# Empty tiles that shift where matmul operands start in SBUF, and another tile order in layer 1

## The chip, the core and the metric

The kernel runs on one core of one Trainium2 chip. The metric is the device time of one execution in microseconds (us), the median of several runs. TensorE (PE in the rows) multiplies, VectorE (DVE), ScalarE (ACT) and GpSimd (POOL) do the elementwise work, and every DMA is issued from the queue of SyncE (SP). SBUF holds 128 partitions; a tile has one start offset, the same in every partition, and everything below on offsets speaks of that byte address within a partition.

## The reference

Two layers of a decoder trunk on 1024 tokens of width 1024, in float32:

```python
for l in range(DEPTH):                      # DEPTH = 2
    mk, mv = memory keys and values of layer l, from rms_norm(mem)
    h = rms_norm(x, norm_mix_g[l])
    if l == 0:   # one projection: conv channels | memory queries
        mix = concat(conformer_conv(u[..., :1536] + b), memory_attention(qm, mk, mv))
    else:        # one projection: NSA queries | memory queries | gates
        mix = concat(nsa_attention(q, gates, *shared), memory_attention(qm, mk, mv))
    x = x + mix @ w_out[l]
    x = x + square(relu(rms_norm(x, norm_mlp_g[l]) @ w_mlp_in[l])) @ w_mlp_out[l]
```

`shared` is the keys and values of the three branches of the block-sparse attention (NSA: compressed blocks, selected blocks, sliding window), made once from the stream after layer 0. The MLP is 4096 wide, and most of the arithmetic lies in it.

## The kernel before

**Tiling.** The 1024 tokens are two halves `hf` of 512. Activations lie transposed, 128 channels on the partitions and 512 tokens along the tile, so that 1024 channels are eight tiles `act[kt]`. Every float32 factor is split into a rounded high part and the low rest, both float32r, side by side in one tile of 4096 bytes: `act[kt][:, 0]` high, `act[kt][:, 1]` low; the same for the weights (`hl`), the hidden tiles of the MLP (`hid`), the probabilities (`PT`), and the queries `Q`. One product is then three matmuls, high by high, high by low and low by high (`mm3`, lines 80 to 82). A matmul of 128 by 128 by 512 streams 512 columns of its moving operand (`rhs`) through the array while the stationary operand (`lhsT`) is held; a weight load (PEld) precedes each.

**Which operand moves.** In the first product of the MLP (`ps_i`, lines 452 to 454), in the output projection (`ps_wo`, 411 to 413) and in the projections of layer 0 (`ps_a`, 80 to 82) `act` moves and `hl` stands. In the second product of the MLP (`ps_mo`, 80 to 82) `hid` moves and `hl` stands. In the memory's keys and values (`ps_mkv`, 277 to 279) `hl` moves and `mh` stands. In the projections of the attention (`ps_tok`, 693 to 695; the memory queries of layer 0 at 80 to 82) `hl` moves with 256 columns and `act` stands. In the attention `KS` moves against `Q` (`ps_s`, 1016), `PT` moves against `V` (`ps_o`, 1076 and 1079), and transposes (`ps_t`, 1060) stream `ident` against `prob`.

**Where tiles lie.** Pools are stacked: those on the left from low addresses upwards in the order in which they are opened, those on the right from the top downwards. A pool takes exactly what its tiles need, so each tile's start follows from the sizes of all pools opened before it. The pool `w` (weights, with three `raw` tiles for arriving weights and five `hl` tiles) starts at byte 4928, `hid` follows at 31552, then `tmp`, then `act` at 62464. The slots of `act` serve again as `prob` while the attention of that half runs. Above `act` lie some constants and the residual stream `x`, whose slots also serve as `q`, `mq` and others in the attention. On the right lie the attention's own pools: `wa` (its weights, also called `hl`) and `nsa` (`KS`, `V`, `Q`, `PT`, `sm`, `small`).

**Order.** The program is written with generators, and a scheduler fixes each engine's order when the kernel is built; the engines run their lists in order and meet at semaphores. The stages of PE are: layer 0's projections with the convolution on the other engines (0 to 250 us), output projection and MLP of half 0, then the attention of half 0 and the output projection and MLP of half 1 woven into each other, the attention of half 1 woven into the last MLP of half 0, and at the end output projection and MLP of half 1.

**Layer 1's mixed tiles.** Attention writes its results to DRAM (`mixd`, line 1083): first the memory heads, tiles 6 and 7, then per group of heads tiles 0 to 2 and tiles 3 to 5. `load_mix` (391) reads the eight tiles back in a given order, `w_out` uses them in that order, and the MLP takes the tiles in the same order, since `w_out` puts its result into the slot that came free.

Of the kernel before, what the change touches and what calls it, by code (L numbers as in the profile page):

```python
# [8 lines left out]
F32 = mybir.dt.float32  # L9
# [10 lines left out]
WG = 2  # L20
MIXORD = (4, 5, 6, 7, 0, 1, 2, 3)
MIXORD0 = (0, 1, 2, 3, 4, 5, 6, 7)
SUBP = (0, 2)
ORDER = "B0A1M0X0B1A2A3B2A4B3A5B4B5F0M1Z0G0N1"
MQB = 2
MB = (1, 2)
P = 128
# [359 lines left out]
def load_mix(k, act, src, kts, pool, tag="raw", bufs=2):  # L387

    for kt in kts:
        raw = pool.tile([P, HF], F32, tag=tag, name="mix", bufs=bufs)  # L390
        k.nc.sync.dma_start(raw, src[:, kt])
        split(k.nc, act[kt][:, 0], act[kt][:, 1], raw)
# [237 lines left out]
def mem_dst(mixd, hf):  # L630

    return lambda h, cp: mixd[hf, (h % 2) * 64:(h % 2) * 64 + 64, 6 + h // 2, cp * 256:cp * 256 + 256]
# [280 lines left out]
def nsa(k, pool, psum, hf, q, mq, gate, KcS, Vc, masks, Kd, Vd, kvd, pslot, mem_dst, out):  # L913


    nc = k.nc
# [183 lines left out]
                for j in range(3):  # L1100
                    yield query, scores, (c, g, j, KS, V)

    Q = pend = None
    todo = units()
    unit = next(todo)
    while unit:
        now, unit = unit, next(todo, None)
        Q = Q or now[0](*now[2])
        nextQ = unit and unit[0](*unit[2])
        p = now[1](Q, *now[2])  # L1110
        if pend:
            values(*pend)
        Q, pend = nextQ, p
# [3 lines left out]
def attention(k, hf, x, acc, act, slot, pslot, gate, KcS, Vc, hTA, tail, masks, mixd, kvd, Kd, Vd):  # L1117


    nc, tc, ins = k.nc, k.tc, k.i  # L1120
    h = act
    with tc.tile_pool(name=f"psa{hf}", bufs=1, space=bass.MemoryType.PSUM) as k.psum, \
            tc.tile_pool(name=f"wa{hf}", bufs=1, side="right") as k.wpool:
        with tc.tile_pool(name=f"na{hf}", bufs=1, side="right") as k.tmp:
            k.start(norm_steps(k, h, x, [acc], None))
            k.flush()
        with tc.tile_pool(name=f"pa{hf}", bufs=1, side="right") as cp:
            steps = cmp_kv(k, cp, h, hf, slot, KcS, Vc, hTA, tail)
            next(steps)
            mq = slot(3, [P, 2, 4, P], F32, "mq")  # L1130
            pss = proj(k, h, [ins["b_wm"][:, kt * 292:kt * 292 + 292] for kt in range(KT)], C_MIX1, 292)
            for cs, ps in pss:
                nc.vector.tensor_add(gate[:, 4 * hf + cs.start], ps[:, 256:292], k.rows[:, R_GB:R_GB + 36])
            gv = gate[:, 4 * hf:4 * hf + 4]
            nc.scalar.activation(gv, gv, AF.Tanh, scale=0.5)
            nc.vector.tensor_scalar(gv, gv, 0.5, 0.5, op0=ALU.mult, op1=ALU.add)
            queries(k, cp, [(cs, ps[:, :256]) for cs, ps in pss], by_pair(mq), k.mqg[:, 1])
            next(steps)
            kv_tok(k, h, hf, cp, 0, Kd, Vd)
            next(steps)  # L1140
            next(steps)
            kv_tok(k, h, hf, cp, 1, Kd, Vd)
            next(steps, None)
            q = [slot(j, [P, 4, 256], F32, "q") for j in range(3)]
            for j in range(3):
                queries(k, cp, proj(k, h, [ins["b_wq"][j, i] for i in range(4)], C_MIX1),
                        [q[j][:, 2 * a:2 * a + 2].rearrange("p c (h d) -> p c h d", d=64) for a in range(2)], k.mqg[:, 2])
    with tc.tile_pool(name=f"nsa{hf}", bufs=1, side="right") as pool, \
            tc.tile_pool(name=f"psn{hf}", bufs=1, space=bass.MemoryType.PSUM) as psum:
        nsa(k, pool, psum, hf, q, mq, gate, KcS[hf], Vc[hf], masks, Kd, Vd, kvd, pslot, mem_dst(mixd, hf), mixd[hf])  # L1150


# [2 lines left out]
def build(tc, ins, out):  # L1155
    nc = tc.nc
    k = K()
# [2 lines left out]

    def pool(es, name, side="left"):
        return es.enter_context(tc.tile_pool(name=name, bufs=1, side=side))

    def psum_pool(name):
        return tc.tile_pool(name=name, bufs=1, space=bass.MemoryType.PSUM)

    with ExitStack() as es:
# [14 lines left out]
        xs = dram.tile([2, P, KT, HF], F32, name="xs")  # L1182
        mixd = dram.tile([2, P, KT, HF], F32, name="mixd")
# [5 lines left out]
        k.hid = pool(es, "hid")  # L1189
        k.tmp = pool(es, "tmp")  # L1190
        k.rpool = k.tmp
        ap = pool(es, "act")

        def act_tiles(hf):
# [46 lines left out]
        hTA = late.tile([P, 2, 64], F32, name="hTA")  # L1241
        tail = late.tile([P, 4, 8], F32, name="tail")
        masks = (late.tile([P, 5 * P], F32, name="edge"), late.tile([P, 8, 64], F32, name="cm"))
        xp = pool(es, "x")

        xslot = [slots(xp, f"x{hf}") for hf in range(2)]
# [69 lines left out]

        act = [act_tiles(hf) for hf in range(2)]
        x = [x_tiles(hf) for hf in range(2)]
        load_mix(k, act[0], mixd[0], MIXORD, k.wpool, "raw", k.nraw)
        k.lo_eng = nc.vector  # L1320
        rs = [w_out(k, 1, act[0], x[0], xs[0], MIXORD)]
        ka.rpool = pool(es, "rb", "right")

        ps3 = es.enter_context(psum_pool("ps3"))
        wb = pool(es, "wb", "right")
        ka.psum, ka.wpool, ka.tmp, ka.tag = ps3, wb, wb, "mm"
        load_mix(ka, act[1], mixd[1], MIXORD, ka.wpool, "mix", 8)
        rs.append(w_out(ka, 1, act[1], x[1], xs[1], MIXORD))
        for hf in range(2):
            if hf == 1:  # L1330
                k.psum, k.nps = ps3, 4
            mlp(k, 1, x[hf], act[hf], rs[hf], lambda o: nc.sync.dma_start(out[hf, :, o], x[hf][o]), MIXORD)
        k.flush()


# [66 lines left out]
```

## Time and profile before

| | us |
|---|---|
| median of 3 runs | 2460.57 (2460.16 to 2464.42) |
| the profiled execution, its own time | 2463.4 |
| its span, first to last instruction | 2461.6 |
| PE busy in the span | 2372.0 (96%) |
| DVE, ACT, POOL busy | 1649.2, 1326.1, 1143.4 |
| share of PE in the chain of work that ended last | 85% |
| share of DVE, DMA and ACT in it | 6%, 3%, 2% |

Busy time of PE is the union of its instructions, each drawn with its whole latency (0.39 us for a matmul of 512 columns), while a new one starts every 0.23 us. How fast PE goes is therefore not read from the busy time but from the distance between the starts of neighbouring matmuls, which the list of instructions in order of time gives to 0.01 us; over a run of n steps the mean is good to 0.01 us / n.

### The profile page before, as it was taken

Reading aid. Unit: us, or ns where it says so; the run is one execution under the profiler, and the core shown is the slowest. Engines: PE = TensorE matmul, PEld = TensorE weight load, DVE = VectorE, ACT = ScalarE, POOL = GpSimd, SP = SyncE. Lnnn points to the kernel's source line nnn. Section 1 sums busy time; section 2 is a strip of 40 time slices with the busy share of each in tenths; the row PEclk is TensorE's granted clock in tenths of the full one; section 3 lists DMA queues with packets and bytes.
Section 4 is the critical chain, followed back from the end, with each engine's and each line's share of the span. In section 5 each row is a group of like instructions: output and inputs, shape, how many; then the busy total and the mean of one; then the engine's idle time right before and its main releaser. Section 6 shows DMA issues by size and latency. Waiting matters only on the chain.

```text
span 2461.6 us, 36812 instructions
## 1 busy us (share of the span) xinstructions
PE 2372.0 (96%) x12098; PEld 1994.3 (81%) x12098; DVE 1649.2 (67%) x3598; ACT 1326.1 (54%) x3002; POOL 1143.4 (46%) x1004
## 2 busy tenths in 40 slices
PE   5998999999998999999999899999999997999999
PEld 4887687888787988888787798888888886888887
DVE  7897576998677567877436856778777864433333
ACT  5575555333556567776434665766667653433332
POOL 2876544544401356565440125566565650344443
PEclk9999999999998999999999999999999998999999
DMA  5212433323344342222335442322222225233233
GB/s 185 80 53 84 153 96 101 101 91 95 122 143 141 97 122 81 88 83 78 115 103 165 145 131 86 107 65 67 81 81 62 66 66 183 78 94 97 92 95 102
DMA packets 157214, 250.87 MB, mean 102 GB/s; under 512 B 17632, under 2 KB 48992, under 8 KB 156512
## 3 DMA queue, kind: packets, MB, share of 16 engines
q1 hardware_dynamic: 157024, 248.52, 32.3%
q8 instruction: 96, 1.57, 0.3%
q14 instruction: 94, 0.77, 0.1%
HBM read 217.52 MB, written 20.45 MB: 97 GB/s over the span
## 4 chain that ended last, share of the span: by engine, by line
PE 85%; DVE 6%; DMA 3%; issue 3%; ACT 2%; POOL 1%; SPq 0%; POOLq 0%; ACTq 0%; DVEq 0%
PE ps_i L452 9%; PE ps_i L453 9%; PE ps_i L454 9%; PE ps_mo L80 9%; PE ps_mo L82 8%; PE ps_mo L81 8%; PE ps_t L1060 4%; PE ps_s L1016 4%; PE ps_o L1076 2%; PE ps_wo L411 2%; PE ps_o L1079 2%; PE ps_wo L412 2%; PE ps_wo L413 2%; PE ps_a L80 2%; PE ps_a L82 2%
## 5 line engine op out<-in xcount | busy, mean ns | idle before, releaser
L112 POOL TENSOR_TENSOR hl<-raw,hl 128x512 fp32r<-128x512 f32 x540 | 696.2, 1300 | 759.0 <-ACT hl L111 736.4
L111 ACT ACTIVATE hl<-raw 128x512 fp32r<-128x512 f32 x648 | 405.4, 630 | 630.1 <-PE ps_i L454 251.6
L474 DVE TENSOR_TENSOR x<-x,ps_mo 128x512 f32<-128x512 f32 x512 | 348.8, 684 | 139.1 <-PE ps_mo L82 136.2
L452 PE MATMUL ps_i<-act,hl 128*128 128x512 f32 x1024 | 408.6, 399 | 7.4 <-DVE x L415 7.2
L80 PE MATMUL ps_mo<-hid,hl 128*128 128x512 f32 x1024 | 407.4, 398 | 4.9 <-DVE x L474 4.5
L454 PE MATMUL ps_i<-act,hl 128*128 128x512 f32 x1024 | 407.2, 398 | 0.0
L453 PE MATMUL ps_i<-act,hl 128*128 128x512 f32 x1024 | 406.6, 397 | 0.0
L82 PE MATMUL ps_mo<-hid,hl 128*128 128x512 f32 x1024 | 400.8, 391 | 0.0
L81 PE MATMUL ps_mo<-hid,hl 128*128 128x512 f32 x1024 | 400.7, 391 | 0.0
L452 PEld LDWEIGHTS ps_i<-act,hl 128*128 128x128 f32 x1024 | 192.8, 188 | 51.9 <-DVE x L415 7.4
L460 DVE SCALAR_TENSOR_TENSOR a<-ps_i,r 128x512 f32<-128x512 f32 x128 | 88.1, 689 | 214.4 <-PE ps_i L454 199.3
L80 PEld LDWEIGHTS ps_mo<-hid,hl 128*128 128x128 f32 x1024 | 192.3, 188 | 46.5 <-DVE x L474 8.3
L454 PEld LDWEIGHTS ps_i<-act,hl 128*128 128x128 f32 x1024 | 192.7, 188 | 44.8 <-issue 0.2
L453 PEld LDWEIGHTS ps_i<-act,hl 128*128 128x128 f32 x1024 | 192.8, 188 | 43.2 <-issue 0.2
L82 PEld LDWEIGHTS ps_mo<-hid,hl 128*128 128x128 f32 x1024 | 192.3, 188 | 41.1
L81 PEld LDWEIGHTS ps_mo<-hid,hl 128*128 128x128 f32 x1024 | 192.6, 188 | 37.4 <-issue 0.5
L1027 ACT ACTIVATE prob<-ps_s,small 128x512 f32<-128x512 f32 (+3 forms) x240 | 141.5, 591 | 80.3 <-DVE small L1025 50.7
L1046 POOL TENSOR_TENSOR prob<-prob,small 128x1024 f32<-128x1024 f32 (+3 forms) x120 | 181.2, 1535 | 1.7 <-DVE small L1040 1.4
L1068 DVE TENSOR_TENSOR PT<-ps_t,PT 128x512 fp32r<-128x512 f32 (+1 forms) x220 | 147.3, 671 | 43.4 <-ACT PT L1064 41.4
L1064 ACT ACTIVATE PT<-ps_t 128x512 fp32r<-128x512 f32 (+1 forms) x256 | 141.6, 566 | 60.4 <-PE ps_t L1060 56.2
L1016 PE MATMUL ps_s<-KS,Q 128*128 128x512 f32 (+5 forms) x552 | 144.1, 360 | 0.0
L120 POOL TENSOR_TENSOR hl<-raw,hl 128x512 fp32r<-128x512 f32 (+1 forms) x32 | 38.5, 1205 | 219.2 <-ACT hl L118 185.5
(298 smaller groups left out, 4790.6 us busy)
## 6 DMA issues: line engine op xcount, KB each, us to landing
raw<-in_w_mlp_in_dram SPq DMA_DIRECT2D x256, 256.0 KB, 2.8
raw<-in_w_mlp_out_dram SPq DMA_DIRECT2D x256, 256.0 KB, 2.9
raw<-in_w_out_dram SPq DMA_DIRECT2D x64, 256.0 KB, 3.4
Q<-Q SPq DMA_DIRECT2D x160, 64.0 KB, 2.0
raw<-in_cmp_w_dram SPq DMA_DIRECT2D x32, 256.0 KB, 2.9
raw<-in_a_w_dram SPq DMA_DIRECT2D x24, 256.0 KB, 2.8
raw<-in_b_wq_dram SPq DMA_DIRECT2D x24, 256.0 KB, 2.7
mixd<-ev SPq DMA_DIRECT2D x80, 64.0 KB, 2.1
```

Of the source, the lines that this page charges most:

```text
L80: nc.tensor.matmul(ps, lhsT=lh, rhs=rh, start=(i == 0), stop=False)
L81: nc.tensor.matmul(ps, lhsT=lh, rhs=rl, start=False, stop=False)
L82: nc.tensor.matmul(ps, lhsT=ll, rhs=rh, start=False, stop=(i == n - 1))
L111: nc.scalar.activation(hl[:, 0, :n], raw[:, :n], AF.Copy)
L112: k.last_lo = k.lo_eng.tensor_tensor(hl[:, 1, :n], raw[:, :n], hl[:, 0, :n].bitcast(F32), op=ALU.subtract)
L452: nc.tensor.matmul(p_, lhsT=wh, rhs=h[kt][:, 0], start=kt == 0, stop=False)
L453: nc.tensor.matmul(p_, lhsT=wh, rhs=h[kt][:, 1], start=False, stop=False)
L454: nc.tensor.matmul(p_, lhsT=wl, rhs=h[kt][:, 0], start=False, stop=kt == KT - 1)
L474: nc.vector.tensor_add(x[o], x[o], ps)
L1016: nc.tensor.matmul(o_, lhsT=lhs, rhs=rhs, start=(n_ == 0), stop=(n_ == len(mms) - 1))
L1046: nc.gpsimd.tensor_tensor(t, t, sc[:, :, None].to_broadcast([P, 2, t.shape[-1]]), op=ALU.mult)
L1068: nc.vector.tensor_sub(PT[:, 1, :m], Tv[:, :m], PT[:, 0, :m].bitcast(F32))
```

## The change

Empty tiles are put in front of pools, so that what lies behind them starts elsewhere. `lay0`, 832 bytes, comes before `act`; `lay1`, 768 bytes, before `x`; `lay2` and `lay4`, 160 bytes each, before the attention's pools on the right; `lay5`, 544 bytes, inside `nsa`. Nothing reads or writes them. The numbers below are start offsets modulo 1024 bytes as the two built programs have them (low parts, 2048 bytes on, have the same; slices of 128 columns step by 512 bytes).

| tile | before | after | tile | before | after |
|---|---|---|---|---|---|
| hl of pool w, hid, mh | 832 | 832 | Q in the attention | 512 | 832 |
| act, and prob in its slots | 0 | 832 | KS in the attention | 256 | 576 |
| x, q, mq and others in its slots | 256 | 832 | V in the attention | 512 | 832 |
| hl of pool wa (attention) | 992 | 832 | PT, sm | 992 | 832 |
| hl of pool pair (layer 0) | 96 | 96 | ident | 992 | 992 |
| hl of pool wb (last output projection) | 928 | 928 | | | |

Beyond the kilobyte the two sides differ: `hl` and `hid` start 832 bytes past a multiple of 2048, `act` before 1024 and after 1856 past one.

The second edit replaces the order 4, 5, 6, 7, 0, 1, 2, 3 by 0, 1, 2, 3, 6, 7, 4, 5 in `load_mix`, `w_out` and `mlp` of layer 1, for both halves. The diff, cut to its core:

```diff
+MIXORD1 = (0, 1, 2, 3, 6, 7, 4, 5)
...
         nextQ = unit and unit[0](*unit[2])
+        lay = lay or pool.tile([P, 136], F32, name="lay5")
         p = now[1](Q, *now[2])
...
+            tc.tile_pool(name=f"lay2{hf}", bufs=1, side="right") as lay, \
             tc.tile_pool(name=f"wa{hf}", bufs=1, side="right") as k.wpool:
+        lay.tile([P, 40], F32, name="lay2")
...
+    with tc.tile_pool(name=f"lay4{hf}", bufs=1, side="right") as lay, \
+            tc.tile_pool(name=f"nsa{hf}", bufs=1, side="right") as pool, \
...
+        lay.tile([P, 40], F32, name="lay4")
...
+    def lay(es, size, name, side="left"):
+        if size:
+            pool(es, name, side).tile([P, size // 4], F32, name=name)
...
+        lay(es, 832, "lay0")
         ap = pool(es, "act")
...
+        lay(es, 768, "lay1")
         xp = pool(es, "x")
...
-        load_mix(k, act[0], mixd[0], MIXORD, k.wpool, "raw", k.nraw)
+        load_mix(k, act[0], mixd[0], MIXORD1, k.wpool, "raw", k.nraw)
...
-        rs = [w_out(k, 1, act[0], x[0], xs[0], MIXORD)]
+        rs = [w_out(k, 1, act[0], x[0], xs[0], MIXORD1)]
...
-        load_mix(ka, act[1], mixd[1], MIXORD, ka.wpool, "mix", 8)
-        rs.append(w_out(ka, 1, act[1], x[1], xs[1], MIXORD))
+        load_mix(ka, act[1], mixd[1], MIXORD1, ka.wpool, "mix", 8)
+        rs.append(w_out(ka, 1, act[1], x[1], xs[1], MIXORD1))
...
-            mlp(k, 1, x[hf], act[hf], rs[hf], lambda o: nc.sync.dma_start(out[hf, :, o], x[hf][o]), MIXORD)
+            mlp(k, 1, x[hf], act[hf], rs[hf], lambda o: nc.sync.dma_start(out[hf, :, o], x[hf][o]), MIXORD1)
```

Set side by side, the two built programs have on each engine the same instructions in the same order, and every wait names the same semaphore and the same value; only tile names and addresses differ. Two places show the renaming.

SP's queue after the attention of half 1, before: `mixd<-ev` is the attention's last result, the `mix` rows are the loads of layer 1's tiles 4, 5, 6, 7, 0, 1, 2, 3 (the number in `mix` and `ev` is the allocation's), the bracket names the semaphores waited for.

```order
L1083 DMA mixd_74<-ev_18476 64x2x128 [waits DMAHW7_49,DVE_49]
L108 DMA raw_22073<-in_w_mlp_in_dram 128x512 [waits DMAHW0_49,Pool_49]
L1332 DMA out_0_dram<-x02_18500 128x512 [waits DMAHW1_49,DVE_49]
L391 DMA mix_18890<-mixd_74 128x512 [waits DMAHW7_49,DMAHW2_49,Activation_49]
L391 DMA mix_18894<-mixd_74 128x512 [waits DMAHW3_49]
L391 DMA mix_18898<-mixd_74 128x512 [waits DMAHW4_49]
```

The same place after, where the loads are of tiles 0, 1, 2, 3, 6, 7, 4, 5:

```order
L1084 DMA mixd_74<-ev_18505 64x2x128 [waits DMAHW7_49,DVE_49]
L109 DMA raw_22103<-in_w_mlp_in_dram 128x512 [waits DMAHW0_49,Pool_49]
L1345 DMA out_0_dram<-x02_18530 128x512 [waits DMAHW1_49,DVE_49]
L392 DMA mix_18920<-mixd_74 128x512 [waits DMAHW7_49,DMAHW2_49,Activation_49]
L392 DMA mix_18924<-mixd_74 128x512 [waits DMAHW3_49]
L392 DMA mix_18928<-mixd_74 128x512 [waits DMAHW4_49]
```

Nothing moved: the first load still stands behind the last result and still waits for its landing (`DMAHW7`, to the same count).

ACT at the same place, which makes the high parts of the loaded tiles (`act1x` is tile x of half 1), before:

```order
L87 ACTIVATE act14_18494<-mix_18890 128x512
L87 ACTIVATE act15_18495<-mix_18894 128x512
L87 ACTIVATE act16_18496<-mix_18898 128x512
L87 ACTIVATE act17_18497<-mix_18902 128x512
L87 ACTIVATE act10_18490<-mix_18906 128x512
```

And after:

```order
L88 ACTIVATE act10_18520<-mix_18920 128x512
L88 ACTIVATE act11_18521<-mix_18924 128x512
L88 ACTIVATE act12_18522<-mix_18928 128x512
L88 ACTIVATE act13_18523<-mix_18932 128x512
L88 ACTIVATE act16_18526<-mix_18936 128x512
```

Here the tiles have changed places, and the rows have not: the matmuls of `w_out` follow them in the same way, on the same rows of PE's list.

## Rows read from the trace of the kernel before

**Rows 1.** PE by line and shape: count | busy us, mean ns | idle before and releaser.

```profile
L452 PE MATMUL ps_i<-act,hl 128*128 128x512 f32 x1024 | 408.6, 399 | 7.4 <-DVE x L415 7.2 <-DVE x L474 0.3
...
L1076 PE MATMUL ps_o<-PT,V 128*128 128x256 f32 x396 | 105.7, 285 | 0.0
...
L412 PE MATMUL ps_wo<-act,hl 128*128 128x512 f32 x256 | 104.1, 408 | 0.0
...
L694 PE MATMUL ps_tok<-hl,act 128*128 128x256 f32 x320 | 90.0, 282 | 1.0 <-POOL hl L120 1.0
...
L81 PE MATMUL ps_a<-act,hl 128*128 128x512 f32 x192 | 76.8, 400 | 0.0
```

**Rows 2.** Timeline of PE in the last stage, proj_in: start, us, line, tiles.

```profile
2203.78 0.39 PE L452 MATMUL ps_i<-act,hl 128*128 128x512 f32 x1
...
2214.98 0.39 PE L80 MATMUL ps_mo<-hid,hl 128*128 128x512 f32 x1
```

**Rows 3.** Timeline of PE in the same chunk, proj_out.

```profile
2216.81 0.39 PE L82 MATMUL ps_mo<-hid,hl 128*128 128x512 f32 x1
...
2225.65 0.39 PE L82 MATMUL ps_mo<-hid,hl 128*128 128x512 f32 x1
```

**Rows 4.** Timeline of PE, the memory's keys and values in layer 0.

```profile
28.18 0.39 PE L277 MATMUL ps_mkv<-hl,mh 128*128 128x512 f32 x1
...
32.72 0.39 PE L279 MATMUL ps_mkv<-hl,mh 128*128 128x512 f32 x1
```

**Rows 5.** Timeline of PE, the last output projection.

```profile
2062.28 0.39 PE L411 MATMUL ps_wo<-act,hl 128*128 128x512 f32 x1
...
2102.41 0.39 PE L452 MATMUL ps_i<-act,hl 128*128 128x512 f32 x1
```

**Rows 6.** Timeline of PE, memory queries of layer 0, 256 columns.

```profile
84.94 0.28 PE L82 MATMUL ps_tok<-hl,act 128*128 128x256 f32 x1
...
86.07 0.28 PE L80 MATMUL ps_tok<-hl,act 128*128 128x256 f32 x1
...
87.50 0.28 PE L80 MATMUL ps_tok<-hl,act 128*128 128x256 f32 x1
...
88.92 0.28 PE L80 MATMUL ps_tok<-hl,act 128*128 128x256 f32 x1
```

**Rows 7.** Timeline of PE, a projection of the attention, 256 columns.

```profile
753.41 0.28 PE L693 MATMUL ps_tok<-hl,act 128*128 128x256 f32 x1
...
756.25 0.28 PE L693 MATMUL ps_tok<-hl,act 128*128 128x256 f32 x1
```

**Rows 8.** Timeline of PE where attention and MLP are woven, after transposes.

```profile
1710.71 0.40 PE L81 MATMUL ps_mo<-hid,hl 128*128 128x512 f32 x1
...
1711.87 0.63 PE L1016 MATMUL ps_s<-KS,Q 128*128 128x512 f32 x2
...
1713.63 0.39 PE L82 MATMUL ps_mo<-hid,hl 128*128 128x512 f32 x1
...
1714.53 0.28 PE L1076 MATMUL ps_o<-PT,V 128*128 128x256 f32 x1
```

**Rows 9.** Stretches, matmuls of ps_i alone: us, PE busy (count), PEclk granted, DMA.

```profile
440.00:700.00 260.00, 113.61 (x480) 0.99 0.35 110
1160.00:1300.00 140.00, 68.58 (x288) 1.00 0.36 110
1300.00:2050.00 750.00, 197.68 (x768) 0.99 0.31 96
2050.00:2462.00 412.00, 182.42 (x768) 0.98 0.31 101
```

**Rows 10.** Stretches, matmuls of ps_mo alone, same columns.

```profile
1300.00:2050.00 750.00, 208.36 (x804) 0.99 0.31 96
2050.00:2462.00 412.00, 176.83 (x768) 0.98 0.31 101
```

**Rows 11.** SP's queue after the last attention: start, us, issues.

```profile
2042.87 3.65 SPq L391 DMA_DIRECT2D mix<-mixd  x8
```

More of the change, by code (lines that the diff above doesn't have):

```diff
@@ L1101, in units @@
                     yield query, scores, (c, g, j, KS, V)
-    Q = pend = None
+    Q = pend = lay = None
     todo = units()
@@ L1147, in attention @@
                         [q[j][:, 2 * a:2 * a + 2].rearrange("p c (h d) -> p c h d", d=64) for a in range(2)], k.mqg[:, 2])
-    with tc.tile_pool(name=f"nsa{hf}", bufs=1, side="right") as pool, \
+    with tc.tile_pool(name=f"lay4{hf}", bufs=1, side="right") as lay, \
+            tc.tile_pool(name=f"nsa{hf}", bufs=1, side="right") as pool, \
             tc.tile_pool(name=f"psn{hf}", bufs=1, space=bass.MemoryType.PSUM) as psum:
+        lay.tile([P, 40], F32, name="lay4")
         nsa(k, pool, psum, hf, q, mq, gate, KcS[hf], Vc[hf], masks, Kd, Vd, kvd, pslot, mem_dst(mixd, hf), mixd[hf])
```

## The prediction

> **What bounds the kernel now.** I looked first at the chain of work that ended last: PE holds 85% of it, and in the span PE is busy 96%, with no other engine above 67%. So the question is not who waits for whom but how fast PE goes while it goes. The table of PE's groups [rows 1] gives the counts (three lines of a product, equal in number) and shows that PE hardly idles: 7.4 us before L452, nothing before L412 and L81. Its column of means (399, 408, 400 ns) is latency, not pace. For the pace I went to the timeline of PE and divided the distance of two starts by the steps between them, in stretches that hold one product only.
>
> In the last stage, 48 steps of ps_i take 2214.98 - 2203.78 = 11.20 us, 233.3 ns each [rows 2]. In the same chunk, 39 steps of ps_mo take 2225.65 - 2216.81 = 8.84 us, 226.7 ns each [rows 3]. Both are 512 columns, both have `hl` of pool w standing, and neither run contains a wait. At the full 2.4 GHz, which the granted clock of 0.98 to 1.00 shows for such stretches [rows 9], 512 columns are 213.3 ns; the excess is 13.3 ns in one and 20 in the other. What differs is the moving operand: `hid` starts 832 bytes past a KB, `act` at a whole KB.
>
> Three more places let me sort the causes. In ps_mkv `hl` moves and `mh` stands, both at 832: 20 steps in 4.54 us, 227.0 ns [rows 4]. That product sums 24 matmuls in a PSUM bank as ps_i does, so the length of the sum is not what sets the pace. In the last output projection `act` moves at 0 while `hl` stands at 928: 172 steps in 40.13 us, 233.3 ns [rows 5], so shifting the standing operand by 96 bytes does not help a mover at 0. And in the memory queries, 256 columns with `act` standing at 0, three runs follow each other [rows 6]: `hl` moving at 832, 10 steps, 113.0 ns; `hl` of the pair pool moving at 96, 12 steps, 119.2 ns; `hl` at 832 again, but behind the disturbed run, 12 steps, 118.3 ns. So 832 is no guarantee when the other operand lies at 0: a fast pace exists there, and a disturbance can end it. The same shows where attention and MLP are woven: `hid` at 832 on `hl` at 832 goes at 232.0 ns just after transposes (5 steps, 1.16 us) and at 225 ns, give or take 2.5 for rounding, three microseconds on (4 steps, 0.90 us) [rows 8]. I read this as two streams, the moving operand and the next weights, which fall into step when both start 832 past a KB, and need some matmuls to do so.
>
> **The change part by part.** The two programs have the same lists and the same waits, so no work is added or removed; the sum is of paces alone.
>
> First, ps_i in unbroken stretches. From 440 to 700, 1160 to 1300 and 2050 to 2462 us lie 480 + 288 + 768 = 1536 of them [rows 9]. `act` goes from 0 to 832 and stands against the same `hl` as `hid` does, so I take 233.3 - 226.7 = 6.67 ns: 1536 x 6.67 = **10.2 us**.
>
> Second, ps_i elsewhere: 3 x 1024 [rows 1] less 1536 leaves 1536, woven with attention or convolution. In such a stretch busy time per matmul is 197.68 / 768 = 257.4 ns for ps_i and 208.36 / 804 = 259.2 for ps_mo, so `hid` at 832 has no lead there, whereas in the last stage it has 237.5 against 230.2 [rows 9, 10]. These are busy times with latency in them, and ps_mo waits for a bank every six matmuls, so they only say that the lead is smaller. Bounds 0 and 1536 x 6.67 = 10.2; since `prob`, `V`, `Q` and `PT` come to 832 too and disturb less, I take somewhat over half, **6.0 us**.
>
> Third, ps_wo, 3 x 256 = 768, and ps_a, 3 x 192 = 576 [rows 1]. Of these 192 ps_wo stand on `hl` at 928 and 240 ps_a on `hl` at 96 (the second part of five channel tiles, two halves, 24 each); with a mover at 832 no row shows those pairs. The other 912 give 912 x 6.67 = 6.1 us; the 432 give 0 to 2.9, I take half. Together **7.5 us**. Layer 0's ps_a lies on the path, as PE has no idle time before L81 [rows 1].
>
> Fourth, the attention's projections: 3 x 320 = 960 of 256 columns [rows 1], now at 24 steps in 2.84 us, 118.3 ns [rows 7], with `hl` at 992 on `act` at 0; afterwards both at 832. Nearest rows: 113.0 if they fall into step, 118.3 if not [rows 6]. Bounds 960 x 5.3 = 5.1 us and 0; they run long and unbroken, I take **3 us**.
>
> Fifth, `PT` on `V`, 2 x 396 = 792 [rows 1], 992 to 832 and 512 or 0 to 832: at most 792 x 5.3 = 4.2 us, at least 0. They come a few at a time between transposes, whose `ident` stays at 992, so I take **1 us**. Sixth, the 1536 ps_mo of the woven stretches, which now meet fewer strange offsets: from 232.0 to 226.7 [rows 8] for at most half of them, 0 to 4 us, **1.5 us**. Scores and smaller products I leave out; `KS` comes to 576, not 832.
>
> The order of layer 1's tiles is costed at nothing. An early start of the eight loads could be worth at most their issue time, 3.65 us [rows 11], but the first load stands behind the attention's last result and waits for its landing in either program, and no instruction changes its place.
>
> Sum: 10.2 + 6.0 + 7.5 + 3 + 1 + 1.5 = 29.2 us. It all lies on PE, and what is late next has room: DVE is busy 67%, ACT 54%, POOL 46%. The profiled execution took 2463.4 us with a span of 2461.6, 2.8 us over the median of 2460.57; taking 29.2 off the median gives 2431. Low end 10.2 + 6.1 = 16.3 us, 2444; high end 10.2 + 10.2 + 9.0 + 5.1 + 4.2 + 4 = 42.7, 2418.
>
> **The rivals.** *The offset is not the cause.* The fast movers also lie low (`hl` from byte 4928, `hid` and `mh` from 31552) and the slow ones high (`act` from 62464), so the place in SBUF explains [rows 2 to 5] as well, and the shift leaves the place. Against it: in [rows 6] the same low `hl` runs at both paces, so place alone does not fix the pace. Nothing would change then, 2460. The Trainium skill, "TensorE: Matmul & The Clock Gate", Part 2, speaks for this rival: it gives the moving operand and the weight load two independent read ports in SBUF, so that loading weights takes no bandwidth from a running matmul. By that rule no pair of offsets could matter. The same page has 512/2.4 + 2.5 = 215.7 ns from start to start whatever the operands' addresses; [rows 2] and [rows 3] show 233.3 and 226.7, so the traces disagree with its figure, and by two amounts.
>
> *The new pair is a bad one.* `hl` and `hid` start 832 past a multiple of 2048 bytes, `act` after the change 1856 past one, and no row has that. If what counts is the offset in 2 KB, `act` may land where the pair pool's `hl` is: 119.2 ns for 256 columns [rows 6], 238.4 for 512, 5.1 ns more than now. With 3072 + 768 + 576 = 4416 matmuls that is +22.5 us, 2483. It decides as soon as the pace of ps_i rises above 233.3. Against it: the standing slices of `hl` step by 512 bytes through all of 2048 and [rows 3] keeps one pace over them.
>
> *Only unbroken runs gain.* The woven parts, the projections and the odd pairs give nothing: the low end, 2444.
>
> **How the numbers follow.** Forecast together with its lesser form 0.83, no effect 0.10, the bad pair 0.07. The range 2418 to 2444 is that of the forecast with all its bounds and leaves out the other two, 0.17. A measurement of this kernel tells some 0.2%, 4.9 us, from no change, and every sum of the forecast is beyond that: faster 0.83, same 0.10, slower 0.07.
>
> **What would show it.** Right: starts of ps_i in the last stage 226.7 ns apart, like ps_mo's in the same chunk, and the last stage, 412 us before, shorter by about 768 x 6.67 = 5 us; ps_wo at 226.7; the attention's projections near 113. Wrong: ps_i still at 233.3 (offset not the cause), or above (bad pair); or PE at the new pace with new idle time before L452 and L80, which would mean that something else is late next. SP's loads should start as long after the attention's last result as before; if they come earlier, I misread the queue.

## The result, and the profile after

The changed kernel takes 2444.99 us (median of 6 runs, 2443.32 to 2446.60); the kernel before, run beside it, 2462.1 (6 runs, 2460.16 to 2464.42). The ratio is 0.993, 95% interval 0.9918 to 0.9943: 17 us faster, 0.7%. The forecast was 2431, range 2418 to 2444: the direction is right, the gain of 17.1 us is 0.59 of the 29.2 forecast, and the median lies 1 us above the range.

The profiled execution after took 2443.32 us, 20.1 us less than the one before (2463.4), since it was the fastest of its six. Its page: span, busy time of PE, the share of each engine in the chain that ended last, and the first line of ps_i among PE's groups.

```profile
span 2441.5 us, 36812 instructions
...
PE 2347.9 (96%) x12098; PEld 1993.0 (82%) x12098; DVE 1649.0 (68%) x3598; ACT 1323.7 (54%) x3002; POOL 1145.8 (47%) x1004
...
PE 74%; DMA 4%; DVE 4%; issue 2%; ACT 2%; POOL 1%; SPq 0%; ACTq 0%; POOLq 0%; DVEq 0%
...
L453 PE MATMUL ps_i<-act,hl 128*128 128x512 f32 x1024 | 403.7, 394 | 7.5 <-DVE x L416 7.2
```

PE is still busy 96% of the span, and its share of the chain is still by far the largest, if less than the 85% of before. Its busy time fell by 2372.0 - 2347.9 = 24.1 us; the other engines have the work they had. L453, the first line of ps_i (it was L452), went from 408.6 to 403.7 [rows 1], and its idle time stayed (7.4 and 7.5).

The pace is read as before, from starts in the timeline of PE after. Here is one chunk of the last stage, first ps_i, then ps_mo:

```profile
2187.40 0.39 PE L453 MATMUL ps_i<-act,hl 128*128 128x512 f32 x1
...
2198.28 0.39 PE L81 MATMUL ps_mo<-hid,hl 128*128 128x512 f32 x1
...
2208.94 0.39 PE L83 MATMUL ps_mo<-hid,hl 128*128 128x512 f32 x1
```

48 steps of ps_i take 10.88 us, 226.7 ns each, where [rows 2] had 233.3. ps_mo keeps its 226.7 (47 steps, 10.66 us). `act` has come to the pace of `hid`.

Next, from the same timeline, three products that did not do as forecast: the last output projection (`act` at 832 on `hl` at 928), ps_a on the pair pool's `hl` at 96, and a projection of the attention (256 columns, `hl` at 832 moving on `act` at 832).

```profile
78.58 0.39 PE L81 MATMUL ps_a<-act,hl 128*128 128x512 f32 x1
...
83.94 0.40 PE L83 MATMUL ps_a<-act,hl 128*128 128x512 f32 x1
...
824.38 0.28 PE L694 MATMUL ps_tok<-hl,act 128*128 128x256 f32 x1
...
853.78 0.28 PE L696 MATMUL ps_tok<-hl,act 128*128 128x256 f32 x1
...
2045.67 0.39 PE L414 MATMUL ps_wo<-act,hl 128*128 128x512 f32 x1
...
2087.59 0.40 PE L453 MATMUL ps_i<-act,hl 128*128 128x512 f32 x1
```

The output projection has 41.92 us in 179 steps, 234.2 ns, against 233.3 in [rows 5]: nothing gained. ps_a on `hl` at 96 has 5.36 / 23 = 233.0. The projection takes 29.40 / 245 = 120.0 ns, slower than the 118.3 of [rows 7], and so steady that the 10th and the 90th percentile of its steps both are 120.

The stretches of ps_i and ps_mo after; unlike [rows 9, 10], these lines have two more columns behind PE's, the busy time of the weight loads (PEld) and of DVE. ps_i is in the first fence, ps_mo in the second, and each has the woven stretch ahead of the last output projection and then the last stage:

```profile
1284.00:2034.00 750.00, 192.97 (x768) 139.73 (x768) 21.97 (x32) 0.99 0.31 96
2034.00:2441.00 407.00, 177.46 (x768) 144.07 (x768) 22.02 (x32) 0.99 0.32 103
```

```profile
1284.00:2034.00 750.00, 212.23 (x815) 148.53 (x813) 92.90 (x137) 0.99 0.31 96
2034.00:2441.00 407.00, 176.51 (x768) 144.14 (x768) 87.77 (x128) 0.99 0.32 103
```

The granted clock is 0.99 in both, 0.99 and 0.98 before. In the woven stretch ps_i has 192.97 / 768 = 251.3 ns of busy time per matmul, 6.1 less than before (from start to start the mean fell less there, from 236.8 to 232.6 ns); ps_mo has 212.23 / 815 = 260.4, no less than the 259.2 before. In the last stage ps_i fell from 182.42 to 177.46 us, the 5 us that the prediction gave as a sign.

Last, SP's queue at the second edit's place, and the first ps_wo behind it on PE:

```profile
2023.04 0.59 SPq L1084 DMA_DIRECT2D mixd<-ev  x1
...
2027.32 4.08 SPq L392 DMA_DIRECT2D mix<-mixd  x8
...
2033.21 2.42 SPq L109 DMA_DIRECT2D raw<-in_w_out_dram  x3
```

```profile
2040.05 0.79 PE L412 MATMUL ps_wo<-act,hl 128*128 128x512 f32 x1 [13.96 <-ACT hl L112]
```

The kernel before at the same place, ahead of and behind [rows 11], SP and then PE:

```profile
2038.58 0.59 SPq L1083 DMA_DIRECT2D mixd<-ev  x1
```

```profile
2054.90 0.79 PE L411 MATMUL ps_wo<-act,hl 128*128 128x512 f32 x1 [13.24 <-ACT hl L111]
```

The loads start 4.28 us after the issue of the attention's last result, 4.29 before. But the first ps_wo comes 12.73 us after the loads' start, and came 12.03 us after it before.

### The profile page after: what moved, and what is told of

Its sections match the earlier page's. It is cut to its first block, busy times and chain, and to the rows that moved or that the text cites. A ratio compares the mean times of both kernels' runs of the same rounds, so it can differ in the third digit from the quotient of the medians.

```text
span 2441.5 us, 36812 instructions
## 1 busy us (share of the span) xinstructions
PE 2347.9 (96%) x12098; PEld 1993.0 (82%) x12098; DVE 1649.0 (68%) x3598; ACT 1323.7 (54%) x3002; POOL 1145.8 (47%) x1004
## 4 chain that ended last, share of the span: by engine, by line
PE 74%; DMA 4%; DVE 4%; issue 2%; ACT 2%; POOL 1%; SPq 0%; ACTq 0%; POOLq 0%; DVEq 0%
PE ps_i L453 9%; PE ps_i L455 9%; PE ps_mo L81 9%; PE ps_i L454 9%; PE ps_mo L83 8%; PE ps_mo L82 8%; PE ps_t L1061 4%; PE ps_s L1017 4%; PE ps_o L1077 2%; PE ps_o L1080 2%; PE ps_wo L412 1%; PE ps_wo L413 1%; PE ps_wo L414 1%; PE ps_tok L695 1%; PE ps_tok L696 1%
## 5 line engine op out<-in xcount | busy, mean ns | idle before, releaser
L81 PE MATMUL ps_mo<-hid,hl 128*128 128x512 f32 x1024 | 407.9, 399 | 5.1 <-DVE x L475 4.4
L453 PE MATMUL ps_i<-act,hl 128*128 128x512 f32 x1024 | 403.7, 394 | 7.5 <-DVE x L416 7.2
L455 PE MATMUL ps_i<-act,hl 128*128 128x512 f32 x1024 | 402.3, 393 | 0.0
L454 PE MATMUL ps_i<-act,hl 128*128 128x512 f32 x1024 | 401.5, 392 | 0.0
L453 PEld LDWEIGHTS ps_i<-act,hl 128*128 128x128 f32 x1024 | 192.7, 188 | 46.3 <-DVE x L416 7.4
L81 PEld LDWEIGHTS ps_mo<-hid,hl 128*128 128x128 f32 x1024 | 192.7, 188 | 46.2 <-DVE x L475 8.0
L454 PEld LDWEIGHTS ps_i<-act,hl 128*128 128x128 f32 x1024 | 192.9, 188 | 38.4 <-issue 0.2
```

Source lines behind the costliest of these rows:

```text
L81: nc.tensor.matmul(ps, lhsT=lh, rhs=rh, start=(i == 0), stop=False)
L453: nc.tensor.matmul(p_, lhsT=wh, rhs=h[kt][:, 0], start=kt == 0, stop=False)
L454: nc.tensor.matmul(p_, lhsT=wh, rhs=h[kt][:, 1], start=False, stop=False)
L455: nc.tensor.matmul(p_, lhsT=wl, rhs=h[kt][:, 0], start=False, stop=kt == KT - 1)
```

## The experiments

Unless said otherwise each kernel is the kernel before with the edit shown, timed against it. A mean pace for a product is the mean distance of neighbouring starts over the whole trace, steps of over one and a half times the median left out, so that single waits don't enter.

### Act alone

```diff
+        lay(es, 832, "lay0")
         ap = pool(es, "act")
...
+        lay(es, 192, "lay1")
         late = pool(es, "late")
```

> The kernel before, with act alone moved to 832 bytes past a KB (832 empty bytes ahead of act, 192 behind it, so that everything after lies where it would with a whole KB more). Theory A, the pair of act and hl of pool w makes the whole gain: ps_i in unbroken runs goes from 233.3 to 226.7 ns, its starts add up to about 17 us less, ps_wo and ps_a to about 3 us less, and the time is about 20 us under the kernel before, 2442 us. The attention's projections, with hl still at 992, stay at about 118.3 ns. Theory B, the other empty tiles carry a part of the gain (V, PT, Q, x at 832): at least 5 us are missing, 2447 us or more.

2445.1 us (4 runs, 2440.35 to 2447.22), ratio 0.9925 (0.991 to 0.994): the changed kernel's gain. ps_i in the last stage:

```profile
2126.05 0.39 PE L452 MATMUL ps_i<-act,hl 128*128 128x512 f32 x1
...
2136.71 0.39 PE L454 MATMUL ps_i<-act,hl 128*128 128x512 f32 x1
```

47 steps in 10.66 us, 226.8 ns. The mean pace of ps_i over the whole kernel is 229.9 ns, the same as in the changed kernel, and 235.2 before; ps_wo has 231.5 in both. The projections stay at 118.3. So theory A holds, by the paces and by the time that this kernel shares with the changed one; its 2445.1 us lies between the 2442 and the 2447 of the two theories. `lay0` does it, and the empty tiles ahead of `x`, in `nsa` and ahead of it bring no gain that can be seen, in the woven stretches neither. `prob` lies in the slots of `act` and moved with it here, so what its place adds is not shown.

### The order alone

```diff
-        load_mix(ka, act[1], mixd[1], MIXORD, ka.wpool, "mix", 8)
-        rs.append(w_out(ka, 1, act[1], x[1], xs[1], MIXORD))
+        load_mix(ka, act[1], mixd[1], MIXORD1, ka.wpool, "mix", 8)
+        rs.append(w_out(ka, 1, act[1], x[1], xs[1], MIXORD1))
...
```

> The kernel before, with the order 0, 1, 2, 3, 6, 7, 4, 5 of layer 1's tiles and no empty tiles. Theory A, the order does nothing, since the first of the eight loads waits for the landing of the attention's last result in either program: within 2 us of the kernel before. Theory B, the early tiles come sooner: up to 3.65 us faster, the issue time of the eight loads. A loss of some us would mean that the gain of the empty tiles is larger than the 17 us seen.

2464.02 us (10 runs) against 2462.93 (19 runs), ratio 1.0002 (0.9992 to 1.0011). No gain. SP and PE at the place:

```profile
2043.32 3.65 SPq L392 DMA_DIRECT2D mix<-mixd  x8
...
2048.13 3.61 SPq L109 DMA_DIRECT2D raw<-in_w_out_dram  x3
```

```profile
2056.15 0.80 PE L412 MATMUL ps_wo<-act,hl 128*128 128x512 f32 x1 [14.28 <-DMA out_dram<-x]
```

From the loads' start to the first ps_wo it is 12.83 us. Over all traces with the loads at this place, the old order has 11.54 to 12.47 (seven kernels, mean 12.00), the new 12.45 to 12.83 (four, mean 12.70). The new order seems to cost 0.7 us, with ranges that just overlap. What is late there is not a mixed tile but `hl`: the weights of the output projection are issued behind the eight loads, and wait in SP's queue for the landing of some of them (3.61 us for three issues; in this stretch the profile puts 2.1 us of waiting for `mix` loads on this line, and 1.6 us before). The bracket on the first ps_wo names a store, but the weight load in front of it waits 14.71 us for ACT's `hl`.

### Act at 1024

```diff
+        lay(es, 1024, "lay0")
         ap = pool(es, "act")
```

> The kernel before, with act and all that lies behind it 1024 bytes further up, so that the place changes by more than in the changed kernel and the offset in a KB doesn't. Theory A, the offset counts: ps_i stays at 233.3 ns, within 2 us of the kernel before. Theory B, the place of act counts and not its offset (a border lies in the first KB): ps_i goes to 226.7 ns and the time falls by about 17 to 20 us. If what counts is the offset in 2 KB, ps_i also changes its pace, since act then starts 0 past a multiple of 2048.

2461.67 us (10 runs), ratio 0.9996 (0.9986 to 1.0006). ps_i in the last stage:

```profile
2137.92 0.40 PE L452 MATMUL ps_i<-act,hl 128*128 128x512 f32 x1
...
2148.89 0.40 PE L454 MATMUL ps_i<-act,hl 128*128 128x512 f32 x1
```

10.97 / 47 = 233.4 ns, as before. Moving `act` further than the change did alters nothing, so its place as such does not count, and since `act` here starts 0 past 2048 and before 1024 past it, the offset in 2 KB does not either. This takes away the first rival's case.

### Everything at a whole KB

```diff
+        lay(es, 192, "layw")
         k.wpool = pool(es, "w")
...
+        lay(es, 832, "lay0")
         ap = pool(es, "act")
```

> The kernel before, with pool w, hid and act all at whole KBs (192 empty bytes ahead of pool w, 832 ahead of act). Theory A, it is the two operands' equal offsets that count: ps_i and ps_mo both at 226.7 ns in unbroken runs and about 20 us under the kernel before, 2442 us. Theory B, it is the mover's own 832 bytes that count: ps_i stays at 233.3 and ps_mo, ps_mkv go up to 233.3 where they now have 226.7; with about 1536 ps_mo in unbroken stretches that is 10 us or more above the kernel before, 2473 us.

2442.22 us (4 runs, 2441.68 to 2446.87), ratio 0.9919 (0.9904 to 0.9934). ps_mo and then ps_i, both with 0 on 0 (or 512):

```profile
2114.83 0.62 PE L80 MATMUL ps_mo<-hid,hl 128*128 128x512 f32 x2
...
2125.48 0.39 PE L82 MATMUL ps_mo<-hid,hl 128*128 128x512 f32 x1
2125.71 0.39 PE L452 MATMUL ps_i<-act,hl 128*128 128x512 f32 x1
...
2136.36 0.39 PE L454 MATMUL ps_i<-act,hl 128*128 128x512 f32 x1
```

Both run at 10.65 / 47 = 226.6 ns. There is nothing in 832: what counts is that mover and standing operand have the same offset. This is theory A.

### Hid at a whole KB, hl at 832

```diff
+        lay(es, 192, "layh")
         k.hid = pool(es, "hid")
...
+        lay(es, 832, "lay0")
         ap = pool(es, "act")
```

> The kernel before, with hid (and mh) brought from 832 to a whole KB, hl of pool w still at 832 and act at 0: now neither of the two large products has equal offsets. Theory A, the pair of offsets sets the pace: ps_mo goes from 226.7 to 233.3 ns in unbroken runs and loses over all its 3072 what ps_i gained in the changed kernel, about 14 to 17 us; ps_mkv goes from 227 to 233. Time about 2478 us. Theory B, the gain belongs to act alone and not to the pair: ps_mo stays at 226.7, 2462 us.

2474.61 us (4 runs, 2474.49 to 2478.29), ratio 1.0058 (1.0043 to 1.0073): slower by 12.6 us. ps_mo in the last stage:

```profile
2132.99 0.63 PE L80 MATMUL ps_mo<-hid,hl 128*128 128x512 f32 x2
...
2143.95 0.39 PE L82 MATMUL ps_mo<-hid,hl 128*128 128x512 f32 x1
```

10.96 / 47 = 233.2 ns. Its mean pace over the kernel goes from 231.2 to 235.9, 4.7 x 3072 = 14 us; ps_mkv, whose `mh` moved too, goes from 229.5 to 232.8. The gain can be taken back from the other product, at the same price per matmul: theory A.

### Act at 64 and at 192

```diff
         act = [act_tiles(0), []]
+        ap.tile([P, 32], F32, name="pad")
...
+        lay(es, 64, "lay0")
         ap = pool(es, "act")
```

> The kernel before, with act of half 0 at 64 and act of half 1 at 192 past a KB, hl of pool w at 832 (and 320, since slices step by 512). Theory A1, moving and standing operand must start equal modulo 256: half 0 goes at 226.7 ns in ps_i, half 1 at 233.3. Theory A2, equal modulo 128 is enough: both halves at 226.7. Theory A3, equal modulo 512 is needed: both at 233.3 or another slow pace.

ps_i on `hl` at 832, in half 0 (`act` at 64) and in half 1 (at 192):

```profile
437.05 0.39 PE L452 MATMUL ps_i<-act,hl 128*128 128x512 f32 x1
...
447.70 0.39 PE L454 MATMUL ps_i<-act,hl 128*128 128x512 f32 x1
...
2126.76 0.40 PE L452 MATMUL ps_i<-act,hl 128*128 128x512 f32 x1
...
2137.72 0.39 PE L454 MATMUL ps_i<-act,hl 128*128 128x512 f32 x1
```

10.65 / 47 = 226.6 ns and 10.96 / 47 = 233.2. 64 and 832 are equal modulo 256 and not modulo 512; 192 is 128 away. So equal modulo 256 is enough, and modulo 128 is not: theory A1. The time of the one run, 2452.48 us, lies 10 us under the kernel before, between before and after. With the pairs of the other kernels, distances of 32, 64, 96 and 128 bytes modulo 256 all gave 233 to 234 ns in unbroken runs; where one offset holds for the whole run, 512 columns have two paces, not a slope.

### The low part apart from the high part

```diff
-    hl = (pool or k.wpool).tile([P, 2, 512], F32R, tag="hl", name="hl", bufs=4 if pool else k.nhl)
+    hl = (pool or k.wpool).tile([P, 2, 544], F32R, tag="hl", name="hl", bufs=4 if pool else k.nhl)[:, :, :512]
...
+        lay(es, 832, "lay0")
         ap = pool(es, "act")
```

> The kernel before, with hl tiles 256 bytes longer, so that their low part stands 128 bytes (modulo 256) from their high part; high part, hid and act all at 64 modulo 256. In a group of three matmuls (high by high, high by low, low by high) the standing operands are high, high, low. Theory A, a running matmul's mover meets the load of the next weights: only the second of the three (next: low) is slow, 233 ns or more from its start to the next, the first and third near 227. Theory B, the mover meets its own standing operand: only the third is slow. Theory C, the pace is a state of the whole run that takes several matmuls to settle: no clean split, all three between 228 and 234 ns. In each case 2 to 5 ns less than 233.3 in the mean of ps_i, and ps_mo as far above 226.7.

An unbroken run of ps_i:

```profile
441.33 0.39 PE L452 MATMUL ps_i<-act,hl 128*128 128x512 f32 x1
...
452.19 0.40 PE L454 MATMUL ps_i<-act,hl 128*128 128x512 f32 x1
```

10.86 / 47 = 231.1 ns in the mean, and it splits by line: the medians of the step are 227 ns from L452 to the next (standing high, next high), 232 to 233 from L453 (standing high, next low) and 234 from L454 (standing low, next high); ps_mo has the same three values. The one run took 2464.55 us, against 2461.6: the mean pace of ps_i over the kernel fell from 235.2 to 233.3 ns, and that of ps_mo rose from 231.2 to 234.0, which together is 0.9 x 3072 = 2.8 us more. Neither A nor B alone: a step is fast only if the operand that stands and the one that comes next both have the mover's offset. C falls too: the pace is not a state of the whole run, it changes from one matmul to the next. The changed kernel has the second case too: behind steps of 227 ns on the weights of pool w, the last ps_a ahead of the pair pool's weights takes 235. That the third step is slow by its own pair, and not as an aftermath of the second, this run alone does not show.

### Other offsets for the attention's weights

The edit is to the changed kernel: no `lay2` in half 0 (`hl` at 992), 352 bytes in half 1 (640).

```diff
-        lay.tile([P, 40], F32, name="lay2")
+        if hf == 1:
+            lay.tile([P, 88], F32, name="lay2")
```

> The changed kernel, with hl of the attention's weights at 992 in half 0 (no empty tile there) and at 640 in half 1 (352 empty bytes), against act at 832. Changed: 120.0 ns from start to start of the projections at 832 on 832, 118.3 before at 992 on 0. Theory A, the equal offsets make the slow pace of 288 cycles: at 992 or at 640 the projections go at 118.3 or less, and the time is 1 to 2 us under the changed kernel, more if one of the two falls to 113 (480 x 7 = 3.4 us for that half). Theory B, act at 832 as the standing operand makes it: 120.0 in both halves and the same time as the changed kernel.

2445.58 us (4 runs), ratio 0.9931 (0.9916 to 0.9946): the time cannot tell. The paces can: the mean over all 256-column projections fell from 119.7 to 117.6 ns, with 117.3 to 118.7 at 992 and runs of either 113.3 or 117.8 at 640. One of those at 113.3, in half 1:

```profile
1373.27 0.28 PE L695 MATMUL ps_tok<-hl,act 128*128 128x256 f32 x1
...
1383.81 0.28 PE L696 MATMUL ps_tok<-hl,act 128*128 128x256 f32 x1
```

93 steps in 10.54 us, 113.3 ns. So the equal pair was what made 120.0 in the changed kernel, theory A, and `act` at 832 as the standing operand is innocent.

### The odd pairs at 832 too

The changed kernel, with empty tiles ahead of the pair pool and of `wb`, and `hl` of the attention's weights at 640:

```diff
+        left.enter_context(tc.tile_pool(name="layp", bufs=1, side="right")).tile([P, 72], F32, name="layp")
         pr = left.enter_context(tc.tile_pool(name="pair", bufs=1, side="right"))
...
+        lay(es, 96, "layb", "right")
         wb = pool(es, "wb", "right")
```

> The changed kernel, with hl of the pair pool and of wb brought from 96 and 928 to 832 too, and hl of the attention's weights at 640. Theory A: the last output projection falls from 234 to 227 ns (192 matmuls, 1.3 us), the 240 ps_a on the pair pool's hl from 233 to 227 or 228 (1.4 us), the 960 projections from 120.0 to 117 (2.9 us): 5.6 us under the changed kernel, 2439 us. Theory B, these pairs never run long enough without a break to settle: no more than the 2.9 us of the projections, 2442 us.

2444.12 us (4 runs, 2438.47 to 2446.31), ratio 0.9919 (0.9903 to 0.9936): too wide a scatter to tell it from the changed kernel by time. Its paces, ps_a behind the pair pool's weights and the last output projection:

```profile
96.27 0.40 PE L81 MATMUL ps_a<-act,hl 128*128 128x512 f32 x1
...
119.19 0.39 PE L83 MATMUL ps_a<-act,hl 128*128 128x512 f32 x1
...
2041.55 0.39 PE L414 MATMUL ps_wo<-act,hl 128*128 128x512 f32 x1
...
2082.58 0.39 PE L414 MATMUL ps_wo<-act,hl 128*128 128x512 f32 x1
```

22.92 / 101 = 226.9 and 41.03 / 181 = 226.7 ns, where the changed kernel has 233.0 and 234.2. In the mean over all, ps_wo fell from 231.5 to 229.3 and ps_a from 232.9 to 230.6: 2.2 x 768 + 2.3 x 576 = 3.0 us, as theory A has it (2.7). The projections at 640 have 117.8 ns, and 113.3 in one run of half 1. The memory queries of layer 0, both of whose weight tiles are now equal to `act`, went from 118.7 to 119.9 ns, a second case in which the equal pair of 256 columns is the slower one.

### Weights first, and the offset of the attention's weights again

Three runs that build on the one above. The first has the old order of layer 1's tiles and calls `load_mix` from within `w_out`, behind the first two weight loads:

```diff
             w = [weights(k, k.i["w_out"][l, o + i][:, 512 * g:512 * g + 512], P) for i in range(WG)]
+            if then:
+                then = then()
             for kt in kts:
```

> The kernel with all offsets as in the run before this one, the old order 4, 5, 6, 7, 0, 1, 2, 3 of layer 1's tiles, and at the last output projection the residual and the first two weight tiles ahead of the eight mix loads in SP's queue, not behind them. Seen so far: from the first mix load's issue to the first ps_wo 11.9 to 12.2 us in the old order and 12.7 to 12.8 in the new, with hl the last to come. Theory A, the weights' place in SP's queue sets this gap: the first ps_wo comes about 9 us after the first of these issues, and the time is 3 to 4 us under the run with all offsets, 2435 us. Theory B, the mix tiles come late instead, since they now stand behind four transfers: no gain beyond the 0.7 us of the order.

2440.22 us (4 runs, 2438.98 to 2442.74), ratio 0.9905 (0.9889 to 0.9922). The first of these issues on SP, and the first ps_wo on PE:

```profile
2032.94 0.80 SPq L405 DMA_DIRECT2D rs<-xs  x2
```

```profile
2040.80 1.22 PE L414 MATMUL ps_wo<-act,hl 128*128 128x512 f32 x2 [9.15 <-DMA mix<-mixd]
```

The first ps_wo comes 7.9 us after the first of these issues instead of 11.5 to 12.8, and now waits for a mix tile. Theory A for the gap; by time it is 4 us under the run above, within its scatter.

The second moves `hl` of the attention's weights to 960 in half 0 and 768 in half 1:

> The run with weights first, with hl of the attention's weights at 960 in half 0 (128 more than act's 832, modulo 256) and at 768 in half 1 (192 more). Seen so far for the projections of 256 columns on act: equal modulo 256 120.0 ns, 64 apart 117.3, 160 apart 118.3. Theory A, only equal offsets are slow and the rest lie between 117 and 118.5: both halves there, the time within 1 us of the run with weights first, 2440 us. Theory B, some distance lets runs of 256 columns settle at the 113.3 ns that rows of before show for ten steps: one half at 113 to 114, about 2 us less.

2438.02 us (4 runs, 2434.97 to 2440.95). At 960 the projections have 118.6 and 120.0 ns, at 768 they have runs at 113.4 and 113.6 and others at 117.8: theory B for 768, though not for all runs. The 120.0 at 960, 128 bytes from `act`, is as slow as the equal pair, so being apart is not enough. The third has 768 in both halves:

> The run with weights first, with hl of the attention's weights at 768 in both halves. Theory A, the distance of 192 modulo 256 gives 116 ns in half 0 as it did in half 1: projections at 116 in the mean against 117.3 there and 120.0 in the changed kernel, 3.8 us under the changed kernel for these alone; with the odd pairs (3 us) and the weights first (3 to 4 us) about 2436 us, 9 us under the changed kernel. Theory B, half 0 and half 1 differ for another reason: 118 in half 0, 2438 us.

2434.07 us (4 runs, 2432.38 to 2434.58) against 2461.6, ratio 0.9889 (0.9872 to 0.9905): 27.5 us under the kernel before, and below the changed kernel with intervals that don't meet (0.9918 to 0.9943 there). Two of its projections, both at 768 on 832:

```profile
1369.63 0.28 PE L698 MATMUL ps_tok<-hl,act 128*128 128x256 f32 x1
...
1380.20 0.28 PE L699 MATMUL ps_tok<-hl,act 128*128 128x256 f32 x1
...
1450.36 0.28 PE L699 MATMUL ps_tok<-hl,act 128*128 128x256 f32 x1
...
1478.62 0.28 PE L699 MATMUL ps_tok<-hl,act 128*128 128x256 f32 x1
```

10.57 / 93 = 113.7 ns and 28.26 / 240 = 117.8: the same offsets, two paces. In the mean half 0 has 116.7 ns and half 1 115.9: theory A, if less than it hoped for in half 0. And its SP queue:

```profile
2025.88 0.80 SPq L405 DMA_DIRECT2D rs<-xs  x2
2026.73 0.90 SPq L109 DMA_DIRECT2D raw<-in_w_out_dram  x2
2027.68 4.38 SPq L392 DMA_DIRECT2D mix<-mixd  x8
```

```profile
2033.41 1.22 PE L414 MATMUL ps_wo<-act,hl 128*128 128x512 f32 x2 [8.86 <-DMA mix<-mixd]
```

PE's idle time there is 8.86 us, 13.24 before. From the first of these issues to the end of the span it is 2432.8 - 2025.88 = 406.9 us, 414.2 in the changed kernel (2441.5 - 2027.32) and 418.7 before.

## Why the prediction was right in kind and too large

| term | forecast, us | measured, us |
|---|---|---|
| ps_i, unbroken and woven (terms 1, 2) | 10.2 + 6.0 | 5.3 x 3072 = 16.3 |
| ps_wo and ps_a (3) | 7.5 | 3.3 x 768 + 2.1 x 576 = 3.7 |
| attention's projections, with the memory queries (4) | 3 | -1.3 x 1152 = -1.5 |
| PT on V (5) | 1 | 0.2 x 792 = 0.2 |
| ps_mo in woven stretches (6; measured over all 3072) | 1.5 | 0.2 x 3072 = 0.6 |
| order of the tiles | 0 | -0.7 |
| sum | 29.2 | 18.6 |

The measured column is the difference of the mean paces of the two traces, and for the order that of the two waits for the first ps_wo (12.73 and 12.03 us); 18.6 lies between the 17.1 of the medians and the 20.1 of the two profiled executions. A further 1.5 us of the miss is the anchor: the forecast took its 29.2 off 2460.57, the median of three runs, and six runs gave 2462.1. From there the low end of 16.3 us would be 2445.8, and the measured time would lie just inside the range. That the time comes so near to the low end is luck, since term 2 gave 6.3 us more than its bound of zero, and terms 3 and 4 gave 2.4 and 1.5 less than theirs.

**Terms 1 and 2 were right**, in pace and in sum. From start to start, the 1536 unbroken ps_i gained 10.0 us and the 1536 woven ones 6.3 us, 4.1 ns each, although I had read from [rows 9, 10] that `hid` had no lead in the woven stretch: busy times hold latency and waits for a bank, as the prediction said. The 6.0 came out right by a choice within 0 to 10.2, not by an argument.

**Term 3 was mis-sized in both parts**, 7.5 us against 3.7. For the 432 odd pairs I took half of 2.9 us without a row. They gained nothing: 234.2 and 233.0 ns. Moving their `hl` as well gave the 3.0 us. And I priced the other 912 as if all were unbroken: their 3.7 us is 4.1 ns each. In the changed kernel the unbroken groups of 24 ps_a run at 227 to 229 ns on the weights of pool w and at 233 on those of the pair pool; the groups from 117 us on, which other matmuls interrupt, lie between 228 and 240.

**Term 4 had the wrong sign**, 3 us forecast and -1.5 measured. This is the step that failed in kind, and the largest miss: I carried "both at 832 falls into step" from 512 columns to 256, and set its lower bound at zero with [rows 6]. Those rows have `hl` at 832 on `act` at 0, a pair with 64 bytes of distance modulo 256, and no row had an equal pair with 256 columns. With 256 columns the equal pair is the slow one, 120.0 ns against 118.3 before. The rows could have warned me: the stretch of 113.0 ns there was not an equal pair. The bound should have gone below zero, by the same argument that made the second rival.

**Terms 5 and 6** were small and came to nothing; the run with `act` alone shows that `V`, `Q` and `PT` need not have been moved.

**The order** did nothing that time can show, as costed; SP's loads start as long after the last result as before. That the order might still cost some 0.7 us, through the landing of the mix loads and the weights behind them in SP's queue, I had not looked for: I priced only the start of the loads, and the first ps_wo waits for `hl`.

**PE's idle time** was read from lines where it cannot stand. "Nothing before L412 and L81" is true, but these are the second lines of their products, and a product waits before its first. For ps_wo that is L411:

```profile
L411 PE MATMUL ps_wo<-act,hl 128*128 128x512 f32 x256 | 103.5, 412 | 22.7 <-ACT hl L111 13.7 <-ACT act L87 4.5 <-DVE x L474 2.8
```

Of these 22.7 us, 13.24 lie before the last output projection, and the runs with the weights first brought them to 9.15 and 8.86. For ps_a the reading holds: its first line has 0.7 us.

**The rivals.** "The offset is not the cause" is out, by the run at 1024 and by the run at whole KBs. With it goes what I drew from the Trainium skill, "TensorE: Matmul & The Clock Gate", Part 2, which gives the moving operand and the weights read ports of their own, so that loading weights takes no bandwidth from a running matmul. The traces do not bear it out here: unbroken, 512 columns cost 226.7 or 233.3 ns as the offsets are equal or not, and with the low part apart a step is slow (233 ns for 227) though only the next weights lie elsewhere. Whether the two share a port no run shows. "The new pair is bad" is out for 512 columns and came true for 256. "Only unbroken runs gain", 2444, gave nearly the measured time, but not by its mechanism: the woven ps_i did gain, and most of that gain was lost in terms 3 and 4.

## What to carry to other kernels

When PE is the bound and hardly idles, read the distance of starts by product: two products of one shape at two paces point to where their operands lie, and where SBUF has room an empty tile in front of a pool is a free repair (1024 bytes that change no offset cost no time, ratio 0.9996). Here 512 columns wanted mover, standing operand and next standing operand equal modulo 256 bytes, 256 columns were slow with them equal, and 292 columns hardly changed (133.6 ns before, 133.3 after); so try a pair by its shape, one half of the work at one offset and the other half at another, before pricing it. A bound taken from rows of another pair must also be allowed to fall below zero.

## What the runs showed of the hardware

- For 512 columns of float32r there are two paces, 226.7 and 233.3 ns from start to start in unbroken runs at a granted clock of 0.99, the 2.4 GHz level. Equal offsets modulo 256 bytes give the first (0 on 0, 832 on 832, 64 on 832); distances of 32, 64, 96 and 128 give the second. The next standing operand counts too: with it alone 128 bytes away, the step takes 232 to 233 ns.
- For 256 columns, equal offsets give a steady 120.0 ns. Counting from the standing operand to the mover, distances of 64 and 192 give 113.3 to 113.9 in some runs and 117.8 in others; 32 gives 116.7 to 117.8, 128 gives 118.6 and 120.0, 160 gives 117.3 to 118.7, 224 gives 118.3. What picks the pace of a run was not found.
- A transfer on SP's queue is issued late where this program's semaphores make it wait for the landing of transfers ahead of it: putting the residual and two weight loads ahead of eight others brought the first matmul from some 12 us to 7.5 to 7.9 us behind the first issue.
- Why the offset counts modulo 256 bytes stays open; the runs show which pairs are fast, not what collides.
